# A macaron decoder layer on one core: small parameters read transposed by strided DMAs, and p5 of the next tile moved between p6 and p3 at three places of FFN2

## The chip, the core and the metric

The kernel runs on one core of a Trainium2 chip. The core has TensorE (PE) for matmuls, VectorE (DVE), ScalarE (ACT), GpSimd (POOL) and SyncE (SP), each with an in-order queue of instructions; they wait for each other through semaphores. SP issues nearly all loads, and 16 DMA engines carry them out. Matmuls write to eight PSUM banks; everything else lies in SBUF, which has 128 partitions. The metric is the device time of one execution in microseconds, as the median of several runs.

## What is computed

One decoder layer over 512 tokens of width 1024, all in float32:

```
x = x + 0.5 * PostNorm_a(SwiGLU_1(PreNorm_a(x)))
x = x +       PostNorm_b(W_out [HGRN2_heads(h) ; mLSTM_heads(h)]),  h = PreNorm_b(x)
x = x + 0.5 * PostNorm_c(SwiGLU_2(PreNorm_c(x)))
...
def swiglu_ffn(x, w_in, w_out):
    gate, up = jnp.split(x @ w_in, 2, axis=-1)
    return (jax.nn.silu(gate) * up) @ w_out
```

The hidden width of each FFN is 2816. The mixer in the middle needs a few small parameters: the weights and bias of a causal convolution (4 x 512 and 512), the logits of the lower bounds of the forget gates (2 x 512; a softmax over the two rows gives the bounds) and two norm gains of 512.

## The kernel before

**Precision.** Each float32 operand is split into a high part (a cast by ScalarE, line 289 for weights) and a low part (a subtraction by VectorE, line 291). A product of two operands is three matmul passes, high by high, high by low, low by high. In `prod` (line 614) the third pass alone reads the low part of the weight.

**FFN input.** The input projection is cut into 11 tiles (`PAIRS`). A tile has four weight blocks of 512 x 256: a and b are the gate and the up columns for the first half of the input width, c and d the same for the second half. Instead of eight block products a tile needs seven, named p1 to p7, of sums of blocks (a Strassen-like scheme). Each product is 24 matmuls of 128x256. The weights of the products are made in place: blocks are added on VectorE (line 305) after the split of an earlier product has read them. `SUMS` says after which product's split the sums `a += b` and `b += d` of a tile are made; after the split of p5 follows `a += d`, after that of p6 `a += c`. The sums of the input blocks lie in fixed buffers; in the order of instructions `xq_76` is the operand of p5, `xq_77` of p4, `xq_78` and `xq_75` of p1 and p2, and three `sq` buffers those of p6, p3 and p7.

**Results of a tile.** `after` combines the products in PSUM. After p5 VectorE writes p5 minus p1 into a fresh bank (line 633), and p6 adds to that bank. After p6 ScalarE copies the bank to another one (line 665, `c22`), to which p7 adds; p3 then adds to the first bank. So p3 may not start before that copy has been made. p4 adds to the bank of p5; VectorE subtracts p1 from it and ScalarE applies SiLU.

**Order.** `ORDER` (FFN1) and `ORDER2` (FFN2) list the products. For FFN2 the tiles go in the order 0, 1, 2, 3, 4, 5, 9, 6, 7, 8, 10 (`SEQ`). p1 and p2 of the tiles 3, 5, 6, 7, 8 (`ONCE`) are done at the start of FFN2, so that in `ORDER2` three places have p6, p3, p7 of one tile and then p5, p4 directly: from tile 2 to 3, from 6 to 7 and from 7 to 8. At the others a p1 or p2 stands between p6 and p3. The list sets the order in which the code is written; a scheduler then sets the final order of each engine's queue by its own estimate of when things are ready, and may move single instructions.

**Weights in flight.** `weights` plans the loads: each goes to one of two rings of buffers, and is issued when the buffer's last reader is done. SP issues them in a fixed order (line 250), and a load that waits for its buffer holds those behind it. `split` makes high and low part, `feed` keeps four split weights alive: the next high part is written when TensorE has read that of the product four places before.

**Small parameters.** `small_params` is called between the head of FFN1 and its main loop. It loads 36 rows of 128 floats with five DMAs, turns them with one TensorE transpose into 128 partitions x 36 columns (`prm`), and computes the lower bounds from them with seven small VectorE operations and two exponentials on ScalarE.

Of the kernel before, what the change touches and what calls it, by code (L numbers as in the profile page):

```python
# [63 lines left out]
ORDER2 = HEADS2 + ORDER2  # L64
SUMS = {0: (("p1", 0), ("p2", 0)), 1: (("p1", 1), ("p6", 0))}
for _r in range(2, PAIRS):
    _s, _t, _n = SEQ[_r - 1], SEQ[_r], [t for t in SEQ[_r + 1 : _r + 2] if t not in ONCE]
    SUMS[_t] = (("p3", _s) if _t in ONCE else ("p1", _t)), ("p4", _s)
    ORDER2 += [("p5", _t), ("p4", _s)]
    if _r == 2:  # L70

        ORDER2 += [("p2", _t), ("p6", _t)]
    else:
        ORDER2 += [("p6", _t)] + ([("p1", t) for t in _n] if _t in ONCE else [("p2", _t)])
    ORDER2 += [("p3", _t)] + [("p1", t) for t in _n if _t not in ONCE] + [("p7", _t)]

# [42 lines left out]
class Layer:  # L119
# [509 lines left out]
    def after(self, p, t):  # L629
# [5 lines left out]
        if p in ("c2", "e2"):  # L635
            nc.scalar.activation(h0 if p == "c2" else h1, self.two_by(bank[p[0] + "1", t]), AF.Silu)
        elif p in ("c4", "e4"):
            h = h0 if p == "c4" else h1
            self.later.append(lambda: tt(h, self.two_by(bank[p[0] + "3", t]), h, ALU.mult))
        elif p == "p1":  # L640
            self.copied = nc.scalar.copy(h1, self.two_by(bank["p1", t]))
        elif p == "p2":
            nc.scalar.activation(h0, self.two_by(bank["p1", t]), AF.Silu)
        elif p == "p4":
            ps = bank["p5", t]
            tt(self.two_by(ps), self.two_by(ps), h1, ALU.subtract)
            def gate():
                nc.scalar.activation(ps, ps, AF.Silu)
                self.later.append(lambda: tt(h1, self.two_by(ps), h1, ALU.mult))
            if self.second and t in GATED:  # L650
                self.after_next = gate
            else:
                gate()
        elif p == "p5" and t < self.filled:
            u = self.u[t] = self.st("u")
            tt(self.two_by(u), self.two_by(bank["p5", t]), h1, ALU.subtract)
        elif p == "p5":
            q = bank["p6", t] = self.ps()
            tt(self.two_by(q), self.two_by(bank["p5", t]), h1, ALU.subtract)
        elif p == "p6" and t < self.filled:  # L660
            u = self.u[t]
            tt(u, bank["p6", t], u, ALU.add)
        elif p == "p6":
            c22 = bank["p7", t] = self.ps()
            self.c22 = [nc.scalar.copy(c22, bank["p6", t])]  # L665
# [172 lines left out]
    def ffn_in(self):  # L838

        nc = self.nc  # L840
# [3 lines left out]
        for n, (p, t) in enumerate(ORDER2[len(HEADS2) :] if self.second else ORDER[len(HEADS) :]):  # L844
            if n > 14 and n % EVERY == 0 and not self.second:
                self.make_sums()
            if n == 14 and self.second:

                with self.behind(self.pooled):
                    nc.gpsimd.drain()  # L850
            with self.behind(*(self.c22 if p == "p3" and self.second else ())):
                self.feed()
            self.c22 = []
            self.lag()
# [1 line left out]
            self.after(p, t)  # L856
            if t == PAIRS - 1 and p in ("p3", "p7"):
                self.hs.append(self.h_tile(len(self.hs)))
        self.feed()
        self.lag()  # L860

# [389 lines left out]
                    made.append(Item((name, PAIRS - 1, "a"), ()))  # L1251
        return made

    def small_params(self):

        nc = self.nc
        mc = self.cp
        rows = self.sp.tile([36, P], F32, tag="junk", bufs=1, name="rows")
        nc.sync.dma_start(rows[0:16, :], self.conv_w[0].rearrange("j (c p) -> (j c) p", p=P))
        nc.sync.dma_start(rows[16:20, :], self.conv_b[0].rearrange("(c p) -> c p", p=P))  # L1260
        nc.sync.dma_start(rows[20:28, :], self.hgrn_lb_logits.rearrange("r (c p) -> (r c) p", p=P))
        nc.sync.dma_start(rows[28:32, :], self.hgrn_norm[0].rearrange("(c p) -> c p", p=P))
        nc.sync.dma_start(rows[32:36, :], self.mlstm_norm[0].rearrange("(c p) -> c p", p=P))
        pt = self.ps()
        nc.tensor.transpose(pt[:, :36], rows, self.ident[:36, :36])
        nc.vector.tensor_copy(self.prm, pt[:, :36])
        l0, l1 = self.prm[:, 20:24], self.prm[:, 24:28]
        mx, e0, e1 = self.col(4), self.col(4), self.col(4)
        nc.vector.tensor_tensor(mx, l0, l1, op=ALU.max)
        nc.vector.tensor_tensor(e0, l0, mx, op=ALU.subtract)  # L1270
        nc.vector.tensor_tensor(e1, l1, mx, op=ALU.subtract)
        nc.scalar.activation(e0, e0, AF.Exp)
# [687 lines left out]
```

## Time and profile before

| what | us |
|---|---|
| median of three runs | 928.82 (928.33 to 929.39) |
| the profiled execution's own time | 929.37 |
| its span, first to last instruction | 927.70 |
| TensorE busy | 918.1 |
| VectorE busy | 766.5 |
| ScalarE busy | 524.5 |
| GpSimd busy | 183.4 |
| FFN1, its output and the mixer end at about | 592 |
| FFN2 input, main loop | 636 to 809 |
| last matmul ends | 921 |

A busy share is an average over the span; the place of each wait is seen in the timeline and in the chain of waits. Matmuls overlap, so the length of a group of matmuls in the timeline is a little longer than the distance to the next group, and it is the distance that counts. TensorE's instruction stream has one group of weight loads (PEld) beside the matmuls. In rows of the profile buffer numbers are left out: `raw` and `w` stand for many buffers.

### The profile page before, as it was taken

The numbers are of one execution on the slowest core, as the hardware profiler recorded it, in microseconds if no ns is written. First come the engines' busy times: TensorE is split into PE (matmuls) and PEld (weight loads), VectorE is DVE, ScalarE is ACT, GpSimd is POOL, SyncE is SP. The second block draws the span as 40 slices with busy tenths as digits, with TensorE's granted clock in tenths as the row PEclk, the third lists the DMA queues.
The fourth block names the chain that finished last, engine by engine and source line by source line (L and its number), as shares of the span: only waits on it lengthen the run. The fifth ranks groups of instructions, "written<-read, shape, count | busy, mean of one in ns | idle before, by whom it ended". The sixth has DMA issues, their size and how long they took to land.

```text
span 927.7 us, 18311 instructions
## 1 busy us (share of the span) xinstructions
PE 918.1 (99%) x7429; PEld 885.0 (95%) x7429; DVE 766.5 (83%) x994; ACT 524.5 (57%) x751; POOL 183.4 (20%) x252
## 2 busy tenths in 40 slices
PE   9999999999999999999999999999999999999997
PEld 8999999999999999998888888899999999999997
DVE  6899988889887877698757565799898989998886
ACT  7645555557566466956533345595354545756661
POOL 2531112111111045552320310314000000010002
PEclk9999999999999999999999999999999999999999
DMA  9255879776897925898832124352354435278542
GB/s 312 76 164 132 190 200 199 190 154 159 213 280 230 256 70 138 167 192 189 175 75 69 46 91 150 100 183 70 114 160 137 136 114 160 90 225 256 168 149 92
DMA packets 118768, 145.42 MB, mean 157 GB/s; under 512 B 7414, under 2 KB 91418, under 8 KB 118684
## 3 DMA queue, kind: packets, MB, share of 16 engines
q1 hardware_dynamic: 102716, 129.05, 45.4%
q0 software_dynamic: 15680, 14.69, 12.1%
q8 instruction: 58, 0.95, 0.4%
q10 hardware_dynamic: 288, 0.52, 0.2%
q14 instruction: 26, 0.21, 0.1%
HBM read 142.14 MB, written 31.46 MB: 187 GB/s over the span
## 4 chain that ended last, share of the span: by engine, by line
PE 59%; DVE 2%; DMA 1%; issue 1%; ACT 1%; DVEq 0%; POOLq 0%; POOL 0%; ACTq 0%
PE ps L614 19%; PE ps L1005 8%; PE ps L544 6%; PE ps L193 5%; PE ps L195 5%; PE ps L194 5%; PE ps L997 4%; PE ps L1429 2%; PE ps L555 1%; DMA raw<-in_ffn_w_in_dram 1%; PE ps L359 1%; DVE w L291 1%; PE ps L1522 0%; PE ps L1727 0%; PE ps L1700 0%
## 5 line engine op out<-in xcount | busy, mean ns | idle before, releaser
L289 ACT CAST w<-raw 128x1024 fp32r<-128x1024 f32 x246 | 251.3, 1028 | 196.6 <-PE ps L614 91.1
L291 DVE TENSOR_TENSOR w<-raw,w 128x1024 fp32r<-128x1024 f32 x246 | 299.5, 1221 | 30.0 <-ACT w L289 28.7
L614 PE MATMUL ps<-xq,w 128*128 128x256 f32 x2016 | 237.2, 277 | 0.0
L614 PEld LDWEIGHTS ps<-xq,w 128*128 128x128 f32 x2016 | 232.9, 188 | 0.0
L614 PE MATMUL ps<-sq,w 128*128 128x256 f32 x1512 | 178.1, 276 | 0.6 <-DVE ps L633 0.4
L614 PEld LDWEIGHTS ps<-sq,w 128*128 128x128 f32 x1512 | 174.3, 188 | 1.4 <-ACT ps L665 0.8
L305 DVE TENSOR_TENSOR raw<-raw,raw 128x1024 f32<-128x1024 f32 x72 | 89.9, 1252 | 8.5 <-DMA raw<-in_ffn_w_in_dram 6.9
L1005 PE MATMUL ps<-w,hs 128*128 128x256 f32 x672 | 80.9, 276 | 0.0
L997 PE MATMUL ps<-w,hs 128*128 128x256 f32 x672 | 79.2, 276 | 0.0
L1005 PEld LDWEIGHTS ps<-w,hs 128*128 128x128 f32 x672 | 78.3, 188 | 0.0
L193 PE MATMUL ps<-w,xq 128*128 128x512 f32 x192 | 77.9, 407 | 0.1
L997 PEld LDWEIGHTS ps<-w,hs 128*128 128x128 f32 x672 | 77.5, 188 | 0.0
L194 PE MATMUL ps<-w,xq 128*128 128x512 f32 x192 | 74.8, 391 | 0.0
L195 PE MATMUL ps<-w,xq 128*128 128x512 f32 x192 | 74.8, 391 | 0.0
L544 PE MATMUL ps<-xq,w 128*128 128x256 f32 x480 | 55.7, 277 | 0.0
L937 POOL DMA_DIRECT2D f2sums<-in_ffn_w_out_dram x15 | 20.4, 1508 | 177.0 <-DMA f2sums<-in_ffn_w_out_dram 177.0
L544 PEld LDWEIGHTS ps<-xq,w 128*128 128x128 f32 x480 | 54.9, 188 | 0.5 <-issue 0.5
L877 ACT CAST hs<-hf 128x1024 fp32r<-128x1024 f32 x32 | 33.7, 1053 | 28.0 <-PE ps L1005 20.3
L878 DVE TENSOR_TENSOR hs<-hf,hs 128x1024 fp32r<-128x1024 f32 x32 | 39.1, 1222 | 9.0 <-ACT hs L877 8.4
L193 PEld LDWEIGHTS ps<-w,xq 128*128 128x128 f32 x192 | 36.1, 188 | 8.4 <-issue 1.0
L195 PEld LDWEIGHTS ps<-w,xq 128*128 128x128 f32 x192 | 36.1, 188 | 8.1 <-DVE xq L366 0.3
L937 POOL DMA_DIRECT2D f1sums<-f1sums x26 | 21.9, 843 | 108.1 <-DMA f1sums<-in_ffn_w_out_dram 54.7
(275 smaller groups left out, 1217.9 us busy)
## 6 DMA issues: line engine op xcount, KB each, us to landing
raw<-in_ffn_w_in_dram SPq DMA_DIRECT2D x98, 512.0 KB, 5.5
raw<-in_ffn_w_out_dram SPq DMA_DIRECT2D x44, 512.0 KB, 4.6
raw<-in_w_mix_in_dram SPq DMA_DIRECT2D x28, 512.0 KB, 6.1
raw<-f2sums SPq DMA_DIRECT2D x15, 512.0 KB
raw<-f1sums SPq DMA_DIRECT2D x13, 512.0 KB, 7.7
raw<-in_w_mix_out_dram SPq DMA_DIRECT2D x8, 512.0 KB, 3.8
f2sums<-in_ffn_w_out_dram SPq DMA_DIRECT2D x30, 128.0 KB, 5.5
f2sums<-in_ffn_w_out_dram SPq DMA_DIRECT2D x15, 256.0 KB, 5.3
```

Source lines behind the costliest of these rows:

```text
L193: mm(ps, sh, mh, start=start, stop=False, **kw)
L194: mm(ps, sh, ml, start=False, stop=False, **kw)
L195: mm(ps, sl, mh, start=False, stop=stop, **kw)
L289: nc.scalar.copy(hi, raw)
L291: self.low = nc.vector.tensor_tensor(lo, raw, hi.bitcast(F32), op=ALU.subtract)
L305: added = (nc.vector if late else nc.gpsimd).tensor_tensor(o, o, c, op=ALU.add)
L544: mm(ps[:, u0:u1], w[:, a, k, :], self.xop(k, b, u0, u1), start=k + n + m == 0, stop=k == ND - 1 and n == 2, skip_group_check=True,)
L614: self.nc.tensor.matmul(ps[:, c], wb[b][:, k, v], left[d][:, k, :], start=first and a + n + k == 0, stop=n == 2 and k == KH - 1, skip_grou ...
L878: self.nc.vector.tensor_tensor(lo, src, hi.bitcast(F32), op=ALU.subtract)
L937: nc.gpsimd.dma_start(to[:, a:b], v, accum_op=ALU.add)
L997: mm(out, a[kk][:, i * P : (i + 1) * P], w[:, b, kk, QUARTER * v : QUARTER * (v + 1)], start=begin and c == kk == n == 0, stop=kk == 1 and ...
L1005: mm(ps[:, QUARTER * c : QUARTER * (c + 1)], A[a][:, c], B[b], start=begin and c == n == 0, stop=n == 2, skip_group_check=True,)
```

## The change

Two parts. First, the five DMAs of the small parameters read the parameters transposed: each writes its columns of `prm` straight from DRAM, one float at a time (128 partitions x 4 to 16 floats). The rows buffer, the TensorE transpose and its copy are gone. The computation of the lower bounds has moved to a function of its own, which is called in FFN1's main loop after its second product and placed behind a VectorE operation of that product.

Second, at the three places of FFN2 the next tile's p5 is taken from behind p7 and put between p6 and p3, and the sum `a += b` that it needs is made after p6's split instead of p3's. The split that follows is placed behind ScalarE's copy also where the product is p5.

```diff
+for _s, _t in ((2, 3), (6, 7), (7, 8)):
+    ORDER2.remove(("p5", _t))
+    ORDER2.insert(ORDER2.index(("p6", _s)) + 1, ("p5", _t))
+    SUMS[_t] = ("p6", _s), SUMS[_t][1]
...
         elif p == "p5" and t < self.filled:
             u = self.u[t] = self.st("u")
-            tt(self.two_by(u), self.two_by(bank["p5", t]), h1, ALU.subtract)
+            self.tick = tt(self.two_by(u), self.two_by(bank["p5", t]), h1, ALU.subtract)
...
-            with self.behind(*(self.c22 if p == "p3" and self.second else ())):
+            with self.behind(*(self.c22 if p in ("p3", "p5") and self.second else ())):
                 self.feed()
...
+            if n == 1 and not self.second:
+                self.lower_bound()
...
-        rows = self.sp.tile([36, P], F32, tag="junk", bufs=1, name="rows")
-        nc.sync.dma_start(rows[0:16, :], self.conv_w[0].rearrange("j (c p) -> (j c) p", p=P))
...
-        pt = self.ps()
-        nc.tensor.transpose(pt[:, :36], rows, self.ident[:36, :36])
-        nc.vector.tensor_copy(self.prm, pt[:, :36])
+    def lower_bound(self):
+
+        nc, mc = self.nc, self.cp
         l0, l1 = self.prm[:, 20:24], self.prm[:, 24:28]
         mx, e0, e1 = self.col(4), self.col(4), self.col(4)
-        nc.vector.tensor_tensor(mx, l0, l1, op=ALU.max)
+        with self.behind(self.tick):
+            nc.vector.tensor_tensor(mx, l0, l1, op=ALU.max)
...
+    def small_params(self):
+
+        nc = self.nc
+        mc = self.cp
+        for c, w in (
+            (0, self.conv_w[0].rearrange("j (c p) -> p (j c)", p=P)),
+            (16, self.conv_b[0].rearrange("(c p) -> p c", p=P)),
+            (20, self.hgrn_lb_logits.rearrange("r (c p) -> p (r c)", p=P)),
+            (28, self.hgrn_norm[0].rearrange("(c p) -> p c", p=P)),
+            (32, self.mlstm_norm[0].rearrange("(c p) -> p c", p=P)),
+        ):
+            nc.sync.dma_start(self.prm[:, c : c + w.shape[1]], w)
```

What this does to the queues is shown at three places; line numbers of the changed kernel are 5 higher in these parts, and a number behind `ps` names one bank's use. TensorE, from tile 2 to tile 3 of FFN2, before: p6 of tile 2, five matmuls of p5 of tile 3, p3 and p7 of tile 2, the other 19 of p5, p4 of tile 2, p6 of tile 3.

```order
L614 MATMUL ps_7530<-sq_6464,w 128x256 x24
L614 MATMUL ps_7686<-xq_76,w 128x256 x5
L614 MATMUL ps_7530<-sq_6465,w 128x256 x24
L614 MATMUL ps_7616<-sq_6466,w 128x256 x24
L614 MATMUL ps_7686<-xq_76,w 128x256 x19
L614 MATMUL ps_7505<-xq_77,w 128x256 x24
L614 MATMUL ps_7711<-sq_6464,w 128x256 x24
```

The same place on TensorE after the change:

```order
L619 MATMUL ps_7527<-sq_6460,w 128x256 x24
L619 MATMUL ps_7626<-xq_76,w 128x256 x24
L619 MATMUL ps_7527<-sq_6461,w 128x256 x24
L619 MATMUL ps_7612<-sq_6462,w 128x256 x24
L619 MATMUL ps_7502<-xq_77,w 128x256 x24
L619 MATMUL ps_7651<-sq_6460,w 128x256 x24
```

All 24 matmuls of p5 now stand behind p6; the scheduler had already put five of them there. It is the same from tile 6 to 7 and from 7 to 8.

VectorE, from tile 6 to tile 7, before. Line 291 is a split's low half, line 305 an add of blocks, line 633 a sum in PSUM. `raw_8342`, `raw_8343`, `raw_8344` are a, b and d of tile 7, `raw_715_8163` and `raw_714_8162` the weights of p3 and p7 of tile 6, `raw_727_8491` and `raw_728_8492` a and b of tile 8, and `ps_8429` is the bank of p6 of tile 6.

```order
L291 TENSOR_TENSOR w<-raw_713_8161,w 128x1024
L305 TENSOR_TENSOR raw_713_8161<-raw_713_8161,raw_716_8164 128x1024
L291 TENSOR_TENSOR w<-raw_715_8163,w 128x1024
L305 TENSOR_TENSOR raw_8343<-raw_8343,raw_8344 128x1024
L633 TENSOR_TENSOR ps_8429<-ps_8404,hf_6463 128x512
L291 TENSOR_TENSOR w<-raw_714_8162,w 128x1024
L305 TENSOR_TENSOR raw_727_8491<-raw_727_8491,raw_728_8492 128x1024
L633 TENSOR_TENSOR ps_8224<-ps_8224,hf_6463 128x512
L291 TENSOR_TENSOR w<-raw_8342,w 128x1024
```

The same place on VectorE after the change; a, b and d of tile 7 are now `raw_8338`, `raw_8339` and `raw_8340`, p3 and p7 of tile 6 read `raw_714_8159` and `raw_713_8158`, a and b of tile 8 are `raw_726_8487` and `raw_727_8488`, and p6's bank is `ps_8426`.

```order
L296 TENSOR_TENSOR w<-raw_712_8157,w 128x1024
L310 TENSOR_TENSOR raw_712_8157<-raw_712_8157,raw_715_8160 128x1024
L296 TENSOR_TENSOR w<-raw_8338,w 128x1024
L310 TENSOR_TENSOR raw_8339<-raw_8339,raw_8340 128x1024
L310 TENSOR_TENSOR raw_8338<-raw_8338,raw_8340 128x1024
L638 TENSOR_TENSOR ps_8426<-ps_8401,hf_6459 128x512
L296 TENSOR_TENSOR w<-raw_714_8159,w 128x1024
L638 TENSOR_TENSOR ps_8220<-ps_8220,hf_6459 128x512
L296 TENSOR_TENSOR w<-raw_713_8158,w 128x1024
L310 TENSOR_TENSOR raw_726_8487<-raw_726_8487,raw_727_8488 128x1024
```

The split of p5 of tile 7 has moved ahead of those of p3 and p7 of tile 6, and the add `a += d` of tile 7 that follows it now stands ahead of the sum for p6 of tile 6.

VectorE in FFN1, right behind the head, before: `prm` is the copy of the transposed rows, and the numbered `col` buffers hold the steps of the lower bounds.

```order
L1266 COPY prm<-ps_635 128x36
L291 TENSOR_TENSOR w<-raw_212,w 128x1024
L1269 TENSOR_TENSOR col_638<-prm 128x4
L291 TENSOR_TENSOR w<-raw_10_123,w 128x1024
L1270 TENSOR_TENSOR col_639<-prm,col_638 128x4
L1271 TENSOR_TENSOR col_640<-prm,col_638 128x4
L633 TENSOR_TENSOR u_695<-ps_670,hf_113 128x512
L291 TENSOR_TENSOR w<-raw_13_126,w 128x1024
```

The same place after the change:

```order
L296 TENSOR_TENSOR w<-raw_212,w 128x1024
L296 TENSOR_TENSOR w<-raw_10_123,w 128x1024
L638 TENSOR_TENSOR u_677<-ps_652,hf_113 128x512
L296 TENSOR_TENSOR w<-raw_13_126,w 128x1024
L638 TENSOR_TENSOR u_706<-ps_681,hf_113 128x512
L1267 TENSOR_TENSOR col_708<-prm 128x4
L296 TENSOR_TENSOR w<-raw_12_125,w 128x1024
L1268 TENSOR_TENSOR col_709<-prm,col_708 128x4
```

The copy is gone, and the first reader of `prm` now stands behind the sums of p5 of tiles 1 and 2 (`u_677`, `u_706`). On SP the five DMAs stand where they stood, and the order of all other queues is the same.

More of the change, by code (lines that the diff above doesn't have):

```diff
@@ L1252, in ffn_items @@
         return made
-    def small_params(self):
-        nc = self.nc
-        mc = self.cp
-        rows = self.sp.tile([36, P], F32, tag="junk", bufs=1, name="rows")
[L1259 to L1263, printed above, removed]
-        pt = self.ps()
-        nc.tensor.transpose(pt[:, :36], rows, self.ident[:36, :36])
-        nc.vector.tensor_copy(self.prm, pt[:, :36])
+    def lower_bound(self):
+        nc, mc = self.nc, self.cp
         l0, l1 = self.prm[:, 20:24], self.prm[:, 24:28]
         mx, e0, e1 = self.col(4), self.col(4), self.col(4)
-        nc.vector.tensor_tensor(mx, l0, l1, op=ALU.max)
+        with self.behind(self.tick):
+            nc.vector.tensor_tensor(mx, l0, l1, op=ALU.max)
         nc.vector.tensor_tensor(e0, l0, mx, op=ALU.subtract)
```

## Prediction

> **What bounds the kernel now.** I read the page's first part, then the waits and the timeline of TensorE, then the chain of waits backwards from the places where TensorE stands. Columns of a timeline: start in us, length in us, engine, line, operation, count, and in brackets idle time before and what ended it.
>
> ```profile
> span 927.7 us, 18311 instructions
> PE 918.1 (99%) x7429; PEld 885.0 (95%) x7429; DVE 766.5 (83%) x994; ACT 524.5 (57%) x751; POOL 183.4 (20%) x252
> ...
> 785.00:921.00 136.00, 136.00 (x1201) 135.87 (x1199) 119.38 (x157) 81.69 (x125) 11.93 (x24) 1.00 0.54 163
> 921.00:928.00 7.00, 0.07 (x1) 0.00 (x0) 2.60 (x5) 0.47 (x2) 0.82 (x2) 0.76 0.40 150
> ```
>
> TensorE (PE, the first figure after each stretch's length) is busy 99% of the span, and from 785 us to the last matmul at 921 us it has no hole at all. So time is won only where TensorE waits or does less, and whatever it wins reaches the end, as long as the other engines are started by it. The granted clock is 1.00. What can be won is small, so I look for every TensorE gap near the change.
>
> ```profile
> PEld ps L614 <- ACT ps L665: 0.8, 3, 0.3
> ```
>
> Three times weight loads of line 614 wait for the ScalarE copy of line 665, 0.8 us in all. That copy saves the sum after p6 before p3 adds to the same bank. The three places, on TensorE:
>
> ```profile
> 673.41 2.88 PE L614 MATMUL ps<-sq,w 128*128 128x256 f32 x24
> 676.13 0.73 PE L614 MATMUL ps<-xq,w 128*128 128x256 f32 x5
> 676.95 5.72 PE L614 MATMUL ps<-sq,w 128*128 128x256 f32 x48
> 682.51 5.04 PE L614 MATMUL ps<-xq,w 128*128 128x256 f32 x43
> 687.38 1.86 PE L614 MATMUL ps<-sq,w 128*128 128x256 f32 x15
> ...
> 752.77 2.88 PE L614 MATMUL ps<-sq,w 128*128 128x256 f32 x24
> 755.49 0.73 PE L614 MATMUL ps<-xq,w 128*128 128x256 f32 x5
> 756.31 5.72 PE L614 MATMUL ps<-sq,w 128*128 128x256 f32 x48
> 761.87 5.04 PE L614 MATMUL ps<-xq,w 128*128 128x256 f32 x43
> 767.29 3.06 PE L614 MATMUL ps<-sq,w 128*128 128x256 f32 x24 [0.39 <-DVE ps L633]
> 770.19 0.75 PE L614 MATMUL ps<-xq,w 128*128 128x256 f32 x5
> 771.01 5.73 PE L614 MATMUL ps<-sq,w 128*128 128x256 f32 x48
> 776.58 5.04 PE L614 MATMUL ps<-xq,w 128*128 128x256 f32 x43
> 781.45 0.73 PE L614 MATMUL ps<-sq,w 128*128 128x256 f32 x5
> ```
>
> A product is 24 matmuls; undisturbed it takes 676.13 - 673.41 = 2.72 us from start to start, 0.1133 us a matmul. At the first place five matmuls of the next tile's p5 already stand between p6 and p3. They cover 5 x 0.1133 = 0.57 us, and p3 starts 0.82 us after them. That is the measure of the gap.
>
> **The change, part by part.**
>
> *FFN2 order.* From 673.41 to 687.38 stand five products: 13.97 us against 5 x 2.72 = 13.60. The stall costs 0.37 us (0.25 of standing and 0.12 of a slower restart). From 752.77 to 781.45 stand ten products: 28.68 against 27.20, so 1.48 us. Of these the two further stalls of the same kind are 2 x 0.37 = 0.74, and the wait for VectorE at 767.29 with its restart is the other 0.74. With the whole p5 between p6 and p3, 2.72 us of matmuls lie over the copy instead of 0.57. The copy itself is ready by 0.82 us, so all three stalls go: 3 x 0.37 = 1.11 us.
>
> The wait at 767.29 is p6 of tile 7 waiting for the sum that VectorE makes from p5 of tile 7. In the new order p5 of tile 7 is complete three products earlier relative to that p6, with p3, p7 of tile 6 and p4 of tile 6 in between, so that wait has 8.2 us of cover: 0.74 us more.
>
> What can be late instead is p5's weight, and what stands in front of it in VectorE's queue:
>
> ```profile
> 743.14 1.23 DVE L305 TENSOR_TENSOR raw<-raw,raw 128x1024 f32<-128x1024 f32 x1 [1.06 <-DMA raw<-in_ffn_w_in_dram]
> ...
> 748.41 1.22 DVE L291 TENSOR_TENSOR w<-raw,w 128x1024 fp32r<-128x1024 f32 x1
> 749.55 1.22 DVE L305 TENSOR_TENSOR raw<-raw,raw 128x1024 f32<-128x1024 f32 x1
> 750.68 0.69 DVE L633 TENSOR_TENSOR ps<-ps,hf 128x512 f32<-128x512 f32 x1
> 751.29 1.22 DVE L291 TENSOR_TENSOR w<-raw,w 128x1024 fp32r<-128x1024 f32 x1
> 755.44 1.23 DVE L305 TENSOR_TENSOR raw<-raw,raw 128x1024 f32<-128x1024 f32 x1 [2.94 <-DMA raw<-in_ffn_w_in_dram]
> ```
>
> The row at 743.14 adds b to a of tile 7, the moment b has landed; its load is not moved. The split at 748.41 becomes that of p5 of tile 7 instead of p3 of tile 6; its low half is needed in the third pass, at 755.49 + 16 x 0.1133 = 757.30, so 7 us are to spare. But the next add to tile 7 (a += d) now stands ahead of the row at 750.68, which makes the sum that p6 of tile 6 starts from. One add is 750.68 - 749.55 = 1.13 us, so that row ends at 750.68 + 1.13 + 0.69 = 752.50. TensorE starts that p6 at 752.77; at 767.29 it began 0.15 after the row it had waited for, so ready is 752.65. The margin is 0.12 us, by far the thinnest here. I take 0.1 us for it, between 0 and 0.74 (a stall like that of 767.29).
>
> Later, the add of b to a of tile 8 waits for a load (the row at 755.44). That load goes into the buffer which the split of p3 of tile 6 frees:
>
> ```profile
> 749.66 5.66 DMA raw<-in_ffn_w_in_dram
> ...
> 767.15 0.14 issue
> 767.29 3.08 PE ps L614 x24
> ```
>
> In the new queue this split comes after p5's split, two adds and the sum, at 748.41 + 3 x 1.13 + 0.61 = 752.4: it ends at 753.6 instead of 749.63, the load lands near 753.6 + 5.66 = 759.3, and VectorE stands from about 755.3 to 759.3, 4.0 us instead of 2.94. Behind that add are the split of p4 of tile 6 (ends 762.4 after add 1.13, a sum 0.60 and itself 1.22; needed in p4's third pass, 763.65 + 1.81 = 765.46) and the sum for p6 of tile 7 (ends 763.1, needed 766.37). Slack 3 us: I cost this at nothing, and it is covered until the load is 3 us later still. The queues of SP and POOL keep their order; the loads of c of tile 8 and of tile 10 that queue behind move by about 4 us as well, and their users stand 5 us or more later.
>
> At the first place VectorE works without a gap, but p5's operand was summed long before, and its split simply trades places with that of p3, which then has 4 us to spare. Nothing for that.
>
> *Small parameters.* TensorE loses one instruction:
>
> ```profile
> 43.40 2.88 PE L614 MATMUL ps<-xq,w 128*128 128x256 f32 x24
> 46.21 0.25 PE L1265 MATMUL ps<-ident,rows 36*128 36x36 f32 x1
> 46.39 5.72 PE L614 MATMUL ps<-xq,w 128*128 128x256 f32 x48
> 51.95 1.30 PE L614 MATMUL ps<-sq,w 128*128 128x256 f32 x10
> ```
>
> From 43.40 to 51.95 are three products and the turn: 8.55 - 8.16 = 0.39 us. All of it goes. VectorE loses a 0.18 us copy; its nine small operations move a few rows down, and ScalarE's table load and two exponentials move behind two casts: off TensorE's path, where the splits concerned are 1.6 us or more ahead of use. I put 0 on that, bounded by 0.3 each way.
>
> The DMAs now fetch 36 x 128 = 4,608 single floats instead of 36 rows. SP and the transfers:
>
> ```profile
> 21.77 1.39 SPq L1259 DMA_DIRECT2D rows<-in_conv_w_dram  x1
> 28.75 0.36 SPq L160 DMA_DIRECT2D gpost<-in_norm_post_dram  x1
> 54.16 9.71 SPq L250 DMA_DIRECT2D raw<-in_ffn_w_in_dram  x6
> ...
> rows<-in_conv_w_dram SPq DMA_DIRECT2D x1, 8.0 KB, 7.1
> DMA packets 3, 0.03 MB, mean 2 GB/s; under 512 B 0, under 2 KB 0, under 8 KB 0
> DMA packets 1614, 0.32 MB, mean 127 GB/s; under 512 B 1056, under 2 KB 1614, under 8 KB 1614
> ```
>
> The last row but one is the stretch from 33 to 54 us: three packets, the queues are empty, and SP issues nothing between 29.1 and 54.16. The last is 353.0 to 355.5 us, where 1,024 pieces of 32 bytes (a strided load of line 1504) go through 16 engines in 2.5 us: at most 16 x 2.5 / 1056 = 0.038 us of an engine each. So 4,608 pieces take at most 4,608 x 0.038 / 16 = 10.9 us. They start as the rows do and the rows land by 21.77 + 7.1 = 28.9, so they are there by 40. The first reader, VectorE's maximum, now stands behind the sum of p5 of tile 2, whose product ends at 51.95. Hidden with 12 us to spare; cost 0, and no gain.
>
> The Trainium skill (DMA: Bandwidth & Descriptors, section Rules for kernel authors) says that a strided last dimension becomes one descriptor per element, and warns of a plain DMA with a rearranged pattern in place of a transpose: a factor of 19. If the factor were on the price above, the estimate by that page would be 207 us instead of 10.9, and the kernel's time near 1,100 us. No run here shows 4-byte pieces in number; the 32-byte row speaks against it.
>
> **The sum.** 1.11 + 0.74 + 0.39 - 0.1 = 2.1 us. The profiled execution took 929.37 us (span 927.70 and 1.67 around it) and would take 927.3; it lies 0.55 above the median of the three runs, 928.82. Against the median: 928.82 - 2.1 = 926.7 us. 0.2%, about what a measurement of this kernel tells from no change, is 1.86 us: faster is below 926.96.
>
> **The rivals.**
> - *Part of it comes back as a new wait.* p6 of tile 6 waits for its sum because the load at 743.14 lands half a microsecond later, or a VectorE row slips; or what TensorE wins at 46 us is lost again where VectorE runs without a gap from 656 to 700 us. For: the 0.12 us margin. Against: those chains are started by TensorE and move with it. One stall of 0.4 to 0.74, or 0.39 lost: 927.1 to 928.0.
> - *The order changes nothing.* VectorE and the loads bound the stretch 743 to 767, and TensorE waits elsewhere for what it no longer waits for here. Then only 0.39, perhaps with one 0.37, is won: 928.1 to 928.4.
> - *Slower: the loads of tile 8 come too late.* The point is 3 us beyond the 759.3 above. If that load and those behind it need 10 us instead of 5.66, with VectorE's in-order queue standing, p4 of tile 6 and then p5 of tile 8 each wait: 1.3 us at the first and about as much at the next two splits, 4 us less the 1.9 won: 930.9.
> - *Slower: the single floats are late.* 3,584 of them, up to the logits, must pass in 51.95 - 28.9 = 23 us, 224 on each engine: it decides from 0.103 us each. At 0.2 us VectorE would stand until 73.7 and TensorE, with three splits (8.2 us) in hand from 51.95, lose some 13 us: 940.
>
> **How the numbers follow.** Forecast (926.0 to 926.96) 0.54; partial return 0.23; nothing changed 0.14; tile 8 late 0.06; floats late 0.03. Faster by over 0.2%: 0.55 with a little of the second case; slower: 0.09; within: 0.36. The low end is the sum without the 0.1, plus 0.5 for VectorE's row at the start and for the spread of runs: 926.0. The high end takes in the second and third case with that spread: 929.0, which leaves out some 2 in 10 with the low side.
>
> **What would show it.** Right: no row of weight loads waiting for the copy's line; p6, p5, p3 at 2.72 us distance at three places; no wait at p6 of tile 7; nothing between the products at 46 us; the last matmul near 919. Wrong: a TensorE wait for VectorE at p6 of tile 6, a VectorE gap over 6 us before tile 8's add, or small packets still running at 52 us.

## The result

| kernel | median us | kernel before beside it | ratio (95% interval) |
|---|---|---|---|
| changed, first group (15 runs each) | 927.44 (926.60 to 928.81) | 928.88 | 0.9984 (0.9978 to 0.9991) |
| changed, second group (11 against 35 runs) | 927.30 (927.06 to 927.81) | 929.08 | 0.9982 (0.9973 to 0.9990) |

The change saves 1.44 and 1.78 us, 0.16 to 0.18%. The forecast was 926.7 with a range of 926.0 to 929.0. The range holds, but it is so wide that the 928.88 of the kernel before lies in it too: it would have held without any gain. The forecast time is 0.6 to 0.7 us too low, and the gain is just inside the 0.2% that the forecast called no change. The profiled execution of the changed kernel is one of the longer of its first group, 928.51 us with a span of 926.8; a second trace (927.12, span 925.3) is shown with the experiments.

The page of the changed kernel, span and busy times; then its waits of TensorE (engine, line, waited for: total us, times, longest):

```profile
span 926.8 us, 18311 instructions
PE 918.0 (99%) x7428; PEld 885.5 (96%) x7428; DVE 765.4 (83%) x993; ACT 523.9 (57%) x751; POOL 184.0 (20%) x252
```

```profile
PE ps L194 <- POOL ones L172: 1.2, 1, 1.2
PE ps L364 <- DVE xn L754: 0.5, 1, 0.5
PE ps L619 <- ACT xq L384: 0.2, 1, 0.2
```

The row on the ScalarE copy (now line 670) is gone, and so is the wait of p6 of tile 7; what is left is at the start of the program. Timeline of TensorE in the changed kernel, at the small parameters, at tiles 2 to 3, at tiles 6 to 8 and at the end:

```profile
43.35 8.32 PE L619 MATMUL ps<-xq,w 128*128 128x256 f32 x72
51.51 4.70 PE L619 MATMUL ps<-sq,w 128*128 128x256 f32 x40
...
673.04 2.88 PE L619 MATMUL ps<-sq,w 128*128 128x256 f32 x24
675.76 2.88 PE L619 MATMUL ps<-xq,w 128*128 128x256 f32 x24
...
686.64 2.88 PE L619 MATMUL ps<-sq,w 128*128 128x256 f32 x24
...
752.06 3.06 PE L619 MATMUL ps<-sq,w 128*128 128x256 f32 x24
754.96 2.99 PE L619 MATMUL ps<-xq,w 128*128 128x256 f32 x24
...
780.40 2.99 PE L619 MATMUL ps<-sq,w 128*128 128x256 f32 x24
783.23 2.98 PE L619 MATMUL ps<-xq,w 128*128 128x256 f32 x24
...
909.12 11.04 PE L1004 MATMUL ps<-w,hs 128*128 128x256 f32 x96
```

Between 43.35 and 51.51 stand three products in 8.16 us, with no transpose: before it was 8.55. At tiles 2 to 3 five products take 686.64 - 673.04 = 13.60 us, exactly 5 x 2.72; before 13.97. So far TensorE is 687.38 - 686.64 = 0.74 us ahead of the kernel before.

At tiles 6 to 8 the order works, but the products are slower. From 754.96 to 783.23 stand ten products in 28.27 us, 2.83 us each instead of 2.72. No wait stands in these rows: behind the start at 752.06 matmuls come every 118 ns instead of every 113. That distance from start to start is called the spacing below. Over the ten products from 752.06 to 780.40 the time is 28.34 us, against 28.68 before and 27.20 without loss. VectorE there:

```profile
751.22 0.69 DVE L638 TENSOR_TENSOR ps<-ps,hf 128x512 f32<-128x512 f32 x1
...
756.82 1.23 DVE L310 TENSOR_TENSOR raw<-raw,raw 128x1024 f32<-128x1024 f32 x1 [2.06 <-DMA raw<-in_ffn_w_in_dram]
...
759.70 0.69 DVE L638 TENSOR_TENSOR ps<-ps,hf 128x512 f32<-128x512 f32 x1
```

The sum for p6 of tile 6 (751.22) ends at 751.91, behind the two adds, and p6 starts at 752.06, 0.15 us later: the start waited for it, by some hundredths of a microsecond, which is too little for a row of waits. The slower spacing begins with this start. The sum for p6 of tile 7 ends at 760.39, 5.9 us ahead of its use. The add for tile 8 waits for its load only to 756.82, not to 759.3.

The small parameters, in SP's rows of the changed kernel, and the stretch from 33 to 54 us (after the mean clock: DMA share, GB/s):

```profile
21.53 1.39 SPq L1290 DMA_DIRECT2D prm<-in_conv_w_dram  x1
22.97 5.40 SPq L1290 DMA_DIRECT2D prm<-in_conv_b_dram  x1
...
29.59 0.51 SPq L1290 DMA_DIRECT2D prm<-in_mlstm_norm_dram  x1
```

```profile
33.00:54.00 21.00, 21.00 (x187) 21.00 (x186) 18.90 (x22) 14.04 (x20) 8.97 (x4) 1.00 0.04 13
```

SP stands 5.4 us at the second of the five issues, and all are issued by 30.1 us. From 33 us on the DMA engines are nearly idle (a share of 0.04), and the first reader, VectorE's maximum, starts at 56.1 us: the floats are there long before it.

### The profile page after: what moved, and what is told of

Same layout as the page of the kernel before. It is cut to its first block, busy times and chain, and to the rows that moved or that the text cites. A ratio compares the mean times of both kernels' runs of the same rounds, so it can differ in the third digit from the quotient of the medians.

```text
span 926.8 us, 18311 instructions
## 1 busy us (share of the span) xinstructions
PE 918.0 (99%) x7428; PEld 885.5 (96%) x7428; DVE 765.4 (83%) x993; ACT 523.9 (57%) x751; POOL 184.0 (20%) x252
## 4 chain that ended last, share of the span: by engine, by line
PE 63%; ACT 0%; DVE 0%; DVEq 0%; POOLq 0%; issue 0%; POOL 0%; ACTq 0%
PE ps L619 23%; PE ps L1012 8%; PE ps L549 6%; PE ps L198 5%; PE ps L200 5%; PE ps L199 5%; PE ps L1004 4%; PE ps L1440 2%; PE ps L560 1%; PE ps L364 1%; PE ps L1533 0%; PE ps L1738 0%; PE ps L1711 0%; PE ps L1486 0%; PE ps L1735 0%; PE ps L1498 0%
```

## The experiments

The two spacings, 113 and 118 ns, gave the first theory: **a late start by 0.1 us at p6 of tile 6 sets a slower spacing, which costs over 1 us.** The rival: the late start costs its 0.1 us, and the slower spacing is of another cause. All times below stand beside runs of the kernel before on the same chip.

| run | median us | kernel before | ratio (95% interval) |
|---|---|---|---|
| parameters alone | 928.99 | 928.98 | 1.0001 (0.9992 to 1.0010) |
| order alone | 927.95 | 928.98 | 0.9988 (0.9980 to 0.9997) |
| without the move at 6 to 7 | 929.99 | 928.98 | 1.0013 (1.0004 to 1.0021) |
| one add behind the sum | 927.72 | 928.98 | 0.9986 (0.9978 to 0.9995) |
| both adds behind the sums | 927.58 | 929.08 | 0.9985 (0.9976 to 0.9993) |
| parameters, add behind the sum | 928.63 | 929.08 | 0.9996 (0.9988 to 1.0005) |
| sum made later | 930.57 | 929.08 | 1.0018 (1.0009 to 1.0026) |
| sum made later, one further run | 929.28 | 928.88 | one run, no interval |
| move at 6 to 7 alone | 928.27 | 928.88 | 0.9994 (0.9985 to 1.0003) |
| parameters loaded three times | 946.44 | 928.88 | 1.0189 (1.0175 to 1.0203) |
| 288 bytes set aside | 946.15 | 928.64 | 1.0185 (1.0168 to 1.0202) |

### The small parameters alone

The kernel before with `lower_bound` and the new `small_params`, without the loop that moves p5.

> The kernel before with the part on the small parameters alone; the order of FFN2 is the old one. My theory: the transpose on TensorE costs 0.39 us (8.55 us for three products and the turn, against 3 x 2.72), the 4,608 single floats are hidden, and the gain is carried to the end: 928.9 - 0.4 = 928.5 us, and in the trace 2.77 us from product to product at 46 us with nothing between. Rival: the 0.39 us is lost again where VectorE has no gap (656 to 700 us), so that the last matmul ends where it did: 928.9 us.

Measured: 928.99 against 928.98. The rival's number. TensorE in this run at tiles 2 to 3, and the VectorE sum that p6 of tile 2 starts from:

```profile
672.52 3.09 PE L615 MATMUL ps<-sq,w 128*128 128x256 f32 x24
...
687.10 2.99 PE L615 MATMUL ps<-sq,w 128*128 128x256 f32 x24
```

```profile
671.76 0.71 DVE L634 TENSOR_TENSOR ps<-ps,hf 128x512 f32<-128x512 f32 x1
```

This execution came to p6 of tile 2 0.89 us earlier than the kernel before (673.41): it was 0.74 us ahead at its first product (10.53 instead of 11.27 us), the missing transpose added 0.36, and 0.21 were lost on the way. There it met VectorE's sum, which ended at 672.47, and from there on the products are slow: five of them take 14.58 us instead of 13.97, and at 687.10 only 0.28 us of the lead is left. So the lead is lost between 656 and 700 us, as the rival says, but most of the loss is the slower spacing after a start that had hardly to wait. Part of it comes back: p6 of tile 7, which waits for VectorE in the old order, starts at 766.62 instead of 767.29, and at 781 us the lead is 0.66 again. For a sum that leaves out where an execution starts, take the stretch from the first to the last matmul of the products (line 614, here 615): it is 805.56 us in this trace and 805.49 in the kernel before. By it, too, the parameters alone gain nothing.

The row of the sum for p6 of tile 2 in the kernel before:

```profile
672.55 0.69 DVE L633 TENSOR_TENSOR ps<-ps,hf 128x512 f32<-128x512 f32 x1
```

It ends at 673.24, and p6 starts 0.17 us later, at 673.41; in the run of the parameters the distance is 0.05. So p6 of tile 2 had a margin of 0.12 us already before the change, as thin as the one that the forecast found at p6 of tile 6.

### The order alone

The kernel before with the loop over the three places and the new condition in `ffn_in`; rows, transpose and copy stay.

> The kernel before with the FFN2 order alone; rows, transpose and copy of the small parameters are as before. My theory: three stalls of 0.37 us and the wait of p6 of tile 7 (0.74 us) go, and 1.2 to 1.3 us of it is lost because p6 of tile 6 starts 0.1 us late and TensorE then keeps 117.8 ns a matmul instead of 113.3 up to 785 us: 928.9 - 0.6 to - 1.85 us, by how often the late start happens, so 927.8 us in the middle. Rival: the order brings nothing at all, and all of the measured 1.4 us came from the parameters: 928.9 us.

Measured: 927.95, 1.03 us below. The order brings most of the gain. Whether the parameters add to it when the order is new, the times do not tell: the intervals of this run and of the whole change overlap. In the first trace of the changed kernel the 0.39 us of the transpose are still there at tile 2 (673.04 against 673.41). In the trace of the order alone neither margin was missed; all ten products at tiles 6 to 8 came at 2.72 us.

### Without the move at tiles 6 to 7

```diff
-for _s, _t in ((2, 3), (6, 7), (7, 8)):
+for _s, _t in ((2, 3), (7, 8)):
```

> The changed kernel without the move at tiles 6 to 7; those of 2 to 3 and 7 to 8 stay. The sum for p6 of tile 6 then stands one add earlier in VectorE's queue, so its start is not late, but the stall of p3 of tile 6 (0.37 us) and the wait of p6 of tile 7 (0.74 us) come back. My theory (the late start sets a slower pace that costs 1.3 us): 0.39 + 2 x 0.37 = 1.1 us below the kernel before, 927.8 us, so within 0.4 us of the changed kernel's 927.4. Rival (no pace, each stall counts by itself): 1.1 us above a changed kernel whose late start costs only 0.1 us, 928.5 us.

Measured: 929.99, 1.0 us above the kernel before: both theories missed it. TensorE and VectorE in its trace:

```profile
673.64 3.10 PE L619 MATMUL ps<-sq,w 128*128 128x256 f32 x24 [0.20 <-DVE ps L638]
...
687.88 2.99 PE L619 MATMUL ps<-sq,w 128*128 128x256 f32 x24
...
753.42 2.88 PE L619 MATMUL ps<-sq,w 128*128 128x256 f32 x24
...
762.53 5.04 PE L619 MATMUL ps<-xq,w 128*128 128x256 f32 x43
768.89 2.98 PE L619 MATMUL ps<-sq,w 128*128 128x256 f32 x24 [1.32 <-DVE ps L638]
...
782.59 2.66 PE L619 MATMUL ps<-sq,w 128*128 128x256 f32 x22
```

```profile
765.66 1.22 DVE L296 TENSOR_TENSOR w<-raw,w 128x1024 fp32r<-128x1024 f32 x1
766.91 1.23 DVE L310 TENSOR_TENSOR raw<-raw,raw 128x1024 f32<-128x1024 f32 x1
768.05 0.69 DVE L638 TENSOR_TENSOR ps<-ps,hf 128x512 f32<-128x512 f32 x1
```

The move at 7 to 8 puts the split of p5 of tile 8 and an add ahead of the sum for p6 of tile 7. TensorE was there at 762.53 + 43 x 0.1133 = 767.40 and started at 768.89, 1.5 us late. The move at 6 to 7 has p5 of tile 7 done three products earlier; with it, in the changed kernel, that sum is ready 5.9 us ahead. So at tiles 6 to 8 the moves are not separate gains: in this trace the one at 7 to 8 costs more than it saves without the other.

That is not the whole of the 1.0 us. From 753.42 to 782.59 stand ten products in 29.17 us, 0.49 more than the 28.68 of the kernel before. The trace has a second loss at tiles 2 to 3: p6 of tile 2 waits 0.20 us for VectorE's sum, the slower spacing follows, and five products take 687.88 - 673.64 = 14.24 us, where the kernel before has 13.97 with its stall and the changed kernel 13.60.

### One add behind the sum

```diff
             for out, other in it.adds:
                 o, c = self.raw[out], self.raw[other]
+                q = [self.q] if out == ("f2", 7, "b") else []
...
-                added = (nc.vector if late else nc.gpsimd).tensor_tensor(o, o, c, op=ALU.add)
+                with self.behind(*q): added = (nc.vector if late else nc.gpsimd).tensor_tensor(o, o, c, op=ALU.add)
...
-            tt(self.two_by(q), self.two_by(bank["p5", t]), h1, ALU.subtract)
+            self.q = tt(self.two_by(q), self.two_by(bank["p5", t]), h1, ALU.subtract)
```

> The changed kernel with one VectorE instruction moved: the add b += d of tile 7 stands behind the sum for p6 of tile 6 and the split of p3, no longer ahead of them. The sum ends 1.13 us earlier, so p6 of tile 6 has a margin of 1.2 us instead of 0.1. My theory: no late start, matmuls keep 113.3 ns from 752 to 785 us (2.72 us a product), and the time is 0.5 to 1.3 us below the changed kernel's 927.4, about 926.6. Rival: the slower pace from 752 us on has another cause (the load on PSUM or SBUF in this stretch), products still take 2.83 us, and only the 0.1 us of the late start is won: 927.3 us.

Measured: 927.72. In the trace the late start is gone and the ten products from 752.29 to 779.49 take 27.20 us: neither the late start nor the slower spacing is there, as the theory has it. But the median is no lower than the 927.44 of the changed kernel, where the theory had 926.6.

### The changed kernel once more, and both adds behind the sums

The second takes `("f2", 3, "b")` into the same condition, so that the add of tile 3 stands behind the sum for p6 of tile 2 as well.

> The changed kernel once more, beside the three others of this group, and for a second trace of it. My theory now: there are two thin margins, p6 of tile 2 at 673 us and p6 of tile 6 at 752 us, each missed in some executions by about 0.1 us, and each miss can leave TensorE at 117.8 ns a matmul for up to 33 us. So the span varies by over 1 us from execution to execution, 1.2 to 1.5 us below the kernel before in the median, and the trace shows a late start at 673 or at 752 us, at both, or at neither. Rival (the slow pace from 752 us on belongs to the new order, whatever the margin): the second trace has 2.83 us a product from 752 to 785 us again.

> The changed kernel with two adds of VectorE moved behind the sums that p6 of tile 2 and p6 of tile 6 start from (b += d of tile 3, and b += d of tile 7 as in the run before). My theory: both margins grow by over 1 us, so no late start and no slow pace in any execution, all terms of the forecast's sum arrive (0.39 + 1.11 + 0.74 = 2.2 us), the median is 2.0 to 2.2 us below the kernel before, and the spread of the times is under 1 us. Rival (the 0.39 us of the parameters is lost at 673 us to the load that releases VectorE at 656 us, not to the add): no better than with one add moved, 1.3 us below the kernel before.

Measured: 927.30 and 927.58. TensorE in the second trace of the changed kernel:

```profile
751.87 2.97 PE L619 MATMUL ps<-sq,w 128*128 128x256 f32 x24
754.67 2.88 PE L619 MATMUL ps<-xq,w 128*128 128x256 f32 x24
...
781.87 2.94 PE L619 MATMUL ps<-xq,w 128*128 128x256 f32 x24
```

And the sum and p6 of tile 6 with both adds moved, VectorE first, then TensorE:

```profile
750.24 0.69 DVE L638 TENSOR_TENSOR ps<-ps,hf 128x512 f32<-128x512 f32 x1
```

```profile
752.29 2.88 PE L619 MATMUL ps<-sq,w 128*128 128x256 f32 x24
...
779.49 2.88 PE L619 MATMUL ps<-sq,w 128*128 128x256 f32 x24
```

In the second trace of the changed kernel p6 of tile 6 is late again (its first product takes 2.80 us, 0.08 more), but now the spacing after it is the fast one: 754.67 to 781.87 are ten products in 27.20 us. So the late start was there in both traces of the changed kernel, and the slower spacing in one. What decides between the two no run shows. With both adds moved the sum ends at 750.93, 1.36 us ahead of p6, and ten products take 27.20 us, 1.48 us less than before: the whole of what the forecast had put on this stretch.

Two things hide this in the medians. The spans are 925.5 us in the median for both kernels, 1.9 below the 927.4 of the kernel before; with both adds moved they reach from 924.8 to 925.7, those of the changed kernel from 925.3 to 926.0 in this group and from 924.8 to 927.0 in the first. So over a whole execution the late start costs nothing that the median span shows. The traces show where the executions differ: the first product starts between 10.40 and 11.53 us in the traces, although no edit touches what stands ahead of it. Counted from the first matmul of the products to the last, the kernel before takes 805.49 us, the changed kernel 804.64 and 803.92, and the kernel with both adds moved 803.34: 2.15 us less, all of the forecast's sum, in the one trace of it.

The second is the time outside the span. It is 1.71 us in the kernel before, 1.78 and 1.76 in the two groups of the changed one and 2.07 with both adds moved (2.03 with one). So the two versions with moved adds give up 0.3 us there, where the profile shows nothing, and do not beat the changed kernel. Why is open.

### The parameters alone, with an add behind the sum

The parameters alone, and the add of tile 3 behind the sum for p6 of tile 2.

> The small parameters alone, on the old order of FFN2, and the add b += d of tile 3 moved behind the sum for p6 of tile 2. My theory: without the move the 0.39 us were lost where p6 of tile 2 waits for that sum at 672.5 us; with it they stay, 0.4 us below the kernel before and 0.4 us below the run of the parameters alone. Rival (the single floats cost somewhere else what the transpose saves): no difference from the kernel before.

Measured: 928.63, 0.45 us below the kernel before, where without the moved add it was nothing. Its own interval includes no change, and the intervals of the two runs overlap, so the times point to the theory and do not prove it. At tiles 2 to 3 the trace is as the theory wants it, TensorE first, then the sum:

```profile
673.59 2.88 PE L615 MATMUL ps<-sq,w 128*128 128x256 f32 x24
...
687.58 2.88 PE L615 MATMUL ps<-sq,w 128*128 128x256 f32 x24
```

```profile
670.32 0.69 DVE L634 TENSOR_TENSOR ps<-ps,hf 128x512 f32<-128x512 f32 x1
```

The sum ends 2.6 us ahead, and five products take 13.99 us, with the one stall that the old order has. But this execution had lost its lead earlier, right behind the place of the old transpose:

```profile
51.36 14.30 PE L615 MATMUL ps<-sq,w 128*128 128x256 f32 x120
65.50 2.99 PE L615 MATMUL ps<-xq,w 128*128 128x256 f32 x24
```

Five products in 14.14 us, 2.83 each: the slower spacing once more, at a third place. So no trace shows the 0.39 us arriving at the end by the parameters alone.

### The sum for p6 of tile 6 made later, twice

```diff
-            self.low = nc.vector.tensor_tensor(lo, raw, hi.bitcast(F32), op=ALU.subtract)
+            for _ in range(1 + 2 * ((("f2", 7, "a"), ("f2", 7, "d")) in it.adds)): self.low = nc.vector.tensor_tensor(lo, raw, hi.bitcast(F32), op=ALU.subtract)
...
-            tt(self.two_by(q), self.two_by(bank["p5", t]), h1, ALU.subtract)
+            with self.behind(*([self.low] if t == 6 else [])): tt(self.two_by(q), self.two_by(bank["p5", t]), h1, ALU.subtract)
```

> The changed kernel with the sum for p6 of tile 6 made one VectorE operation later (1.13 us): the low half of the split of p5 of tile 7 is written three times instead of once, with the same values. My theory: the margin of 0.1 us is all there is, so p6 of tile 6 waits about 1.0 us and the time is 1.0 us above the changed kernel's of this group (up to 1.3 more where the slow pace follows in executions that had none). Rival (TensorE is not bound there, since the late start of 0.1 us was an accident of one execution): 0.2 us or less above it.

> The kernel with the sum for p6 of tile 6 made later, once more, for a second trace. Its times lay in two groups, 1.6 us apart (spans of 927.2 to 927.9 and of 928.8 to 930.6), and its first trace was of the lower group, with 113.3 ns a matmul after a wait of 2.2 us. My theory: an execution of the upper group has the same wait and then 117.8 ns a matmul up to 785 us, 1.0 to 1.3 us more. Rival (the groups differ in how long p6 of tile 6 waits): the wait is 1.5 us longer and the matmuls keep 113.3 ns.

Measured: 930.57 in the median, and 929.28 in the one further run. TensorE and VectorE in the first trace:

```profile
753.90 2.97 PE L619 MATMUL ps<-sq,w 128*128 128x256 f32 x24 [2.04 <-DVE ps L638]
756.70 2.88 PE L619 MATMUL ps<-xq,w 128*128 128x256 f32 x24
```

```profile
749.65 3.49 DVE L296 TENSOR_TENSOR w<-raw,w 128x1024 fp32r<-128x1024 f32 x3
753.06 0.69 DVE L638 TENSOR_TENSOR ps<-ps,hf 128x512 f32<-128x512 f32 x1
```

The sum came two operations later, not one, as I had written: the split of p3 slipped ahead of it as well. That is 2.26 us, and TensorE stands 2.04 us and starts about 2.2 us late: the margin was below 0.1 us, and nearly every nanosecond on that sum is a nanosecond of the start. The second trace has nearly the same wait (1.9 us) and the same fast spacing. Of the twelve times five are 928.95 to 929.65 and seven 930.54 to 932.27. Both traces are of the lower group. For four of the upper seven the mean granted clock on record is 0.996 or 0.997, for all others of this run 0.998 or 0.999; so a stretch at a lower clock is a likely part of those four, which no trace shows. For the other three the cause is open.

### The move at tiles 6 to 7 alone

The loop runs over `((6, 7),)`; the small parameters are as before.

> The kernel before with the move at tiles 6 to 7 alone; tiles 2 to 3 and 7 to 8, and the small parameters, as before. My theory: of the forecast's terms this place has one stall (0.37 us) and the wait of p6 of tile 7 (0.74 us), less the late start of p6 of tile 6 (0.1 to 0.2 us), so 0.9 to 1.1 us below the kernel before, nearly all that the order brings (1.0 us). Rival (the three places help each other, as tiles 7 to 8 were worse without tiles 6 to 7): 0.4 us or less below the kernel before.

Measured: 928.27, 0.61 us below, with an interval that includes no gain. In the trace:

```profile
752.26 2.95 PE L619 MATMUL ps<-sq,w 128*128 128x256 f32 x24
...
779.90 2.88 PE L619 MATMUL ps<-sq,w 128*128 128x256 f32 x24
```

Ten products take 27.64 us, 1.04 less than before: the stall at tile 6 (0.37), the wait at tile 7 (0.74), less 0.07 for the late start. The trace gives the theory's size; the times alone could not tell it from the rival's.

### The parameters loaded three times, and the bytes alone

```diff
+        more = mc.tile([P, 2 * 36], F32, name="more")
...
+            for n in range(2):
+                nc.sync.dma_start(more[:, 36 * n + c : 36 * n + c + w.shape[1]], w)
             nc.sync.dma_start(self.prm[:, c : c + w.shape[1]], w)
```

> The changed kernel with every one of the five small parameters loaded three times, twice into columns that nobody reads and then into its own: 13,824 single floats instead of 4,608. My theory: in the changed kernel's trace a 4-byte packet takes 9 ns of an engine and SP's five issues 8.4 us in all (21.5 to 30.1 us), so three times as many end SP's issues at about 47 us, still ahead of the weight loads of 54.5 us and of the first reader at 56 us, and the time does not change (927.3 us). Rival (single floats are dear in number, 0.1 us of an engine each): the last would land at 21.5 + 13,824 x 0.1 / 16 = 108 us, VectorE would stand from 56 us on, and the time would be some 40 us longer.

Measured: 946.44, 17.6 us longer than the kernel before: neither theory's number. SP's first and last issue of the parameters in this run:

```profile
20.45 6.78 SPq L1292 DMA_DIRECT2D more<-in_conv_w_dram  x2
...
36.55 0.51 SPq L1293 DMA_DIRECT2D prm<-in_mlstm_norm_dram  x1
```

13,824 floats were issued from 20.45 to 37.06 us, and nobody waited for them. The next run keeps the first line of the diff only.

> The changed kernel with the 288 bytes per partition that the run of three loads set aside for the two further copies, and nothing else: the 4,608 floats are loaded once, as in the changed kernel, and nobody writes or reads the 288 bytes. All that differs is that the buffers laid out behind them, the weights' among them, lie 288 bytes further on. In the run before, 17.5 us were lost evenly from the first matmuls to the last (0.4 us by 18 us, 7 us by 330 us, 18 us by 917 us), long before and after the floats were on their way. My theory: it is the place of the buffers, and this kernel takes 946 us too, so that the 9,216 further floats cost nothing. Rival (the further loads do it, by some lasting effect): 927.3 us.

Measured: 946.15. So the 9,216 further floats cost nothing that can be measured, and 288 bytes of an unused buffer cost 2% against the changed kernel. The same 100 us of FFN2 in the changed kernel and with the bytes set aside (window, its length, TensorE busy and matmuls, weight loads, VectorE, ScalarE, GpSimd, clock, DMA share, GB/s):

```profile
640.00:740.00 100.00, 100.00 (x883) 100.00 (x882) 91.81 (x95) 48.34 (x57) 1.24 (x1) 1.00 0.46 140
```

```profile
640.00:740.00 100.00, 100.00 (x864) 100.00 (x863) 91.41 (x91) 47.97 (x58) 6.54 (x3) 1.00 0.41 122
```

TensorE is busy throughout in both, at a granted clock of 1.00, and does 2% fewer matmuls. With the bytes set aside it depends on the operand:

```profile
102.71 2.90 PE L619 MATMUL ps<-sq,w 128*128 128x256 f32 x24
105.45 3.00 PE L619 MATMUL ps<-xq,w 128*128 128x256 f32 x24
108.29 0.96 PE L619 MATMUL ps<-sq,w 128*128 128x256 f32 x7
```

A product with an operand in `sq` takes 2.74 us, one with an operand in `xq` 2.84. `xq` is laid out ahead of the 288 bytes, the weights `w` behind them. This points to the place of operand and weight to each other as what sets the spacing there; why, no run shows. The 2.84 us are close to the 2.83 of the slower spacing above, and whether the two have one cause is not shown either.

## Why the forecast held, and where it was off

- **Three stalls behind the ScalarE copy, 1.11 us.** Right. All three are gone. At tiles 2 to 3 it is 13.97 - 13.60 = 0.37 us in the trace, as forecast.
- **The wait of p6 of tile 7, 0.74 us.** Right. With the two stalls beside it, it is the 1.48 us between 28.68 and the 27.20 of the run with both adds moved. The cover of 8.2 us was too high: the sum was ready 5.9 us ahead, which is still ample.
- **The thin margin at p6 of tile 6, 0.1 us.** This is the term that was mis-sized. The forecast found the place, the order of VectorE's rows and the margin of 0.12 us; in three of the four traces that have the move at 6 to 7, no delayed sum, no moved add and the old layout (the changed kernel twice, the move at 6 to 7 alone) the margin was missed, by about 0.1 us or less; in that of the order alone it was not. What it left out is what may follow: matmuls at 118 ns instead of 113 up to 784 us. That cost 28.34 - 27.20 = 1.14 us over ten products in the first trace and 0.08 in the second. The upper bound of 0.74, taken from a stall, was too low for it. The term is not what keeps the median above the forecast, though: with both adds moved it is gone, and the median span is the same 925.5 us.
- **The transpose, 0.39 us, and "whatever it wins reaches the end".** The first half is right: 8.55 to 8.16 us. The second is not borne out for the parameters by themselves: alone, they gained nothing. The rival had named 656 to 700 us as the place of the loss. The forecast called the 0.12 us at p6 of tile 6 by far the thinnest margin and put the first place at nothing; p6 of tile 2 had 0.12 us too. VectorE's sum there moved with TensorE, as the forecast had it, but by 0.77 of 0.89 us, and that was enough for a late start with the slower spacing behind it. I call this cause likely and not shown, since in that trace 0.53 us come back at p6 of tile 7, and since the moved add gave 0.45 us back with an interval that includes no gain.
- **The sum.** In the median span of the second group the gain is 1.9 us (927.4 to 925.5) against 2.1; the time outside the span grew by 0.05 to 0.07. The terms add up in the trace with both adds moved (2.15 us from the first product to the last), so the mechanism is right. That the median came 0.6 to 0.7 us short of it has no single term that the runs show to be the cause.
- **The loads of tile 8.** Safer than forecast: the load released VectorE at 756.82 instead of 759.3, and nobody on TensorE noticed. That the move at 7 to 8 leans on the one at 6 to 7 was not in the forecast at all; without that one, tiles 6 to 8 took 0.49 us more than in the kernel before.
- **The single floats.** Right: hidden. The bound of 0.038 us of an engine each was high. Three times as many were issued in 16.6 us, 16.6 x 16 / 13,824 = 0.019 us of an engine each at most. The Trainium skill (DMA: Bandwidth & Descriptors, section Rules for kernel authors) warns of a factor of 19 for a plain DMA with a rearranged pattern in place of a transpose; for 18 KB in an idle stretch the trace does not bear it out as a cost of the kernel.
- **The rivals.** The partial return fits the time (927.1 to 928.0). In the changed kernel it is seen at the first place that it names, p6 of tile 6, with 1.17 us in one trace and 0.19 in the other against its 0.4 to 0.74; at the second place, 656 to 700 us, the runs of the parameters alone and without the move at 6 to 7 show it, and both traces of the changed kernel have 13.60 us for the five products there. That the order changes nothing is out (1.03 us by the order alone), and so are late loads of tile 8 and late floats. The gain of 0.16 to 0.18% falls under "no change", to which the forecast gave 0.36, not under the likeliest case; that it is inside the range is owed to the range's width.
- **The signs.** No row for the copy's line, no wait at tile 7, nothing between the products at 46 us: all as written. The last matmul ended at 909.12 + 11.04 = 920.2 us in the first trace instead of near 919, and at 918.8 in the second. The sign for "wrong", a wait at p6 of tile 6, came true in part.

## What to carry over

When a kernel is 99% TensorE, count for every moved instruction the margin of the next in-order neighbour, and where it is under 0.2 us, expect to miss it in some executions. Moving an add out of the way mended the trace here and not the median time, so measure before you keep such a fix. A gain ahead of a place where another engine is just in time may be lost there: look for that place before you count the gain. Compare a layout's cost before its schedule's: 288 unused bytes cost ten times what this change won.

## What the runs showed of the hardware that I had not expected

- At a granted clock of 1.00 and without any wait in the trace, the same matmuls come at 113 ns or at 118 ns each (2.72 or 2.83 us a product). A start that is late by under 0.1 us can leave TensorE at the slower spacing for over 30 us (752 to 784 us), or leave it at the faster; both were seen at the same instruction of the same kernel.
- Moving the weights' buffers by 288 bytes against `xq` took 18.7 to 18.9 us (946.15 against 927.44 and 927.30), spread over the whole kernel.
- A DMA of 512 single floats can hold SP for 5.4 us behind one of 2,048: the issue of the bias at 22.97 us. The bias read as rows took 0.31 us at 23.21 in the kernel before. What held it no run separates.
